# A hybrid convolution and attention step on one core: values moved beside the last convolution, two mixing tiles turned into a seven-product pair

## The chip, the core and the metric

The kernel runs on one core of a Trainium2 chip. The metric is the device time of one execution in microseconds, lower is better; the time before is 889.69 us, the median of three runs from 889.56 to 890.85. Profiles come from one profiled execution, and times within it are counted from the start of its span.

## The reference

One layer acts on 128 prompt tokens and 512 latent tokens, 640 rows in all, with a model width of 1024. Both groups are modulated, and one wide projection gives everything else:

```python
z = h @ w_in
hy, g_h, qkv, g_a, m = jnp.split(z, [3 * D_HYENA, 4 * D_HYENA, 4 * D_HYENA + 3 * D_ATTN, 4 * D_HYENA + 4 * D_ATTN], axis=-1)
hy = short_conv(hy, conv_w, conv_b)
v_h, x1, x0 = jnp.split(hy, 3, axis=-1)
q, k, v = [t.reshape(B, L, N_HEADS, HEAD_DIM) for t in jnp.split(qkv, 3, axis=-1)]
...
u = v_h * x1
y = jnp.fft.irfft(uf * ff[None], n=n, axis=1)[:, :L]     # long convolution with an implicit filter
y_h = (y + u * d_bias) * x0
...
p_h = (y_h * jax.nn.silu(g_h)) @ w_bh
p_a = (y_a * jax.nn.silu(g_a)) @ w_ba
m_h, m_a = jnp.split(jax.nn.sigmoid(m), 2, axis=-1)
out = (m_h * p_h + m_a * p_a) @ w_out
x = layer_norm(ALPHA * x + gate * out)
```

y_a is softmax attention with 16 heads: the latent tokens see a window of 8 rows by 16 columns and a cache of 128 context keys, the prompt sees itself. The prompt's keys and values (new_k, new_v) are outputs too.

## The kernel before

**Tiles.** Activations lie transposed: the modulated input h as eight slabs of 128 channels by 640 tokens, split into a high part hH and a low part hL. A weight tile is 1024 by 128 and gives 128 channels of one projection. A product is made of three passes (high by high weight, low by high weight, high by low weight), so a plain tile is 8 slabs x 3 passes x 2 halves of 320 tokens = 48 matmuls of 320 columns. The tile numbers are constants: queries from 32, keys from 40, values from 48, attention gates T_GA from 56, mixing tiles T_MH and T_MA from 64 and 72.

**Pairs.** Two tiles can be made together as a 2 x 2 block product with seven products instead of eight (`pair_tile`). Its products use sums of blocks of h, which are made once, stored to memory (tok_d) and loaded into tiles t2, t3, t1, t4, and sums of weight blocks (s1, s2, s3, s6), which are made per pair by two accumulating transfers on POOL (`summed`) and two additions on DVE (`sum1`, `sum6`). For each product a weight block is split: the high part on ACT (`high`), the low part on DVE (`low`), both into wb, four blocks ahead of PE. The products read, in this order, h, t2, t3, t1, h, t4, h. Each has 4 slabs x 3 passes = 12 matmuls of 320 columns, so a pair has 84 where two plain tiles have 96.

**Stages.** A prologue makes the modulation and h. Then the long convolution runs in four quarters of 256 channels. `weave` sets a list of projections (main) beside the steps of one quarter's convolution (side): `long_conv` forward, `long_conv_back` with the inverse transform (yb, L170 to L172), its transposes on PE (yp, y; L625, L635), the products on DVE (u, L637) and, once both factors are there, the product yu with x0 (`gate_conv`, L471 and L474) that is stored to yu_d. Up to here a scheduler sets the order of the instructions from the order of the program and its own model of their times. The fourth quarter stands beside `hand_over`: the last convolution tiles, values, queries and keys of the first heads, and two mixing tiles (`mix_tile`), whose tanh goes to mh_d. There the pools of the convolution are given up and their memory goes to the attention (`attention_setup`). The tile sg0 of the first gate lies in memory of that kind.

**From the gates on** the order on all engines is the order of the program. `first_gates` makes two plain gate tiles (mm, L182; tanh on ACT L499 and product on DVE L494, into sg0 and sg1), with the split of the first weight blocks between them. Then SP is given: the four copies of a half of h into a contiguous place (hHp, hLp), the loads of the sums of h that are still out, ra1 (the second pair's plain blocks), the bias tiles tm. t2 and t3 are loaded in two halves of two slabs (t2_00 is the high part's first, t2_10 the high part's second, t2_11 the low part's second); the second halves of t2 and t3 wait in the program's text for the convolution's memory. Transfers of SP are put on eight counters in turn, so each transfer also waits until the one eight before it has landed.

**The attention stage** has eight stages; in each, pairs named in a table (HEADS) are the main list, and the steps of one head pair's attention (`attend`) the side list. The pairs of the first stage make the queries and keys of the second heads ("q1") and two gates of the convolution ("h0"). Pairs of later stages make more gates and the mixing tiles ("m"). Their blocks are loaded two pairs ahead (`load_pair(p + 2)`). After it come the projections of both branches, the mixing and the output.

The table that names the pairs, the place of the pairs in the stage, and the gate of the first two tiles:

```python
HEADS = ("q1 h0", "q2 h1 m1", "q3 m2 a2", "q4 h2 m3", "q5 m4 a4", "q6 h3 m5", "q7 a6", "m6 m7")
for _ in mains(j):
    done += 1
    while done in (14, 20, 27) if j == 0 else taken * n_main < done * n_side:
        if next(side, StopIteration) is StopIteration:
            break
```

## Time and profile before

| what | value |
|---|---|
| median of three runs | 889.69 us |
| the profiled execution's own time | 890.32 us |
| its span | 888.5 us |
| instructions | 17140 |
| mean granted clock of the matrix engine | 0.997 |
| last mixing tile, inverse transform, two gates | 347.6 to 354.6, 354.6 to 360.5, 362.2 to 376.6 us |
| first pair | 376.6 to 389.7 us |

PE is the matrix engine, PEld its weight loads, DVE the vector engine, ACT the scalar engine with its function tables, POOL the general engine, SP the engine that issues most transfers. A timeline row gives start, duration, engine, line, operation, output, inputs, shapes and count (x48 joins 48 like instructions), and in brackets the idle time ahead of it with what ended it. A windows row gives the stretch, its length, the engine's busy time and instructions, its mean granted clock, the share of the DMA engines in use, and GB/s. A row of DMA issues gives the size of a transfer and the median time from its issue to its landing.

### The profile page before, as it was taken

How to read it: one execution, taken by the hardware profiler on the slowest of the kernel's cores; microseconds unless marked ns; L12 is line 12 of the kernel's file. 1: busy time of each engine (PE TensorE's matmuls, PEld its weight loads, DVE VectorE, ACT ScalarE, POOL GpSimd, SP SyncE). 2: the span in 40 equal slices, each digit the busy share in tenths (PEclk: the TensorE clock that was granted, in tenths of full speed). 3: DMA queues.
4: the chain of work that ended last, by engine and by line, in shares of the span. 5: the costliest groups of instructions: out<-in, count | busy, mean ns of one | idle time of the engine just before them, and what ended most of it. 6: DMA issues, size and time to landing. Idle time of an engine off the chain costs nothing.

```text
span 888.5 us, 17140 instructions
## 1 busy us (share of the span) xinstructions
PE 869.3 (98%) x6476; PEld 837.8 (94%) x6476; DVE 637.1 (72%) x1215; ACT 450.3 (51%) x956; POOL 192.9 (22%) x216
## 2 busy tenths in 40 slices
PE   8999999999999999999999999999999999999996
PEld 7889999999899999899999999999999999999885
DVE  4897583985687458488867777777877676676666
ACT  4495545644554544467556566666566632243200
POOL 0020001211101021129344334333554200000000
PEclk9999999999999999999999999999999999999998
DMA  8977576878546697798686758665844586446521
GB/s 329 402 211 156 121 158 145 211 197 190 137 100 159 151 222 149 223 337 266 157 248 150 223 154 239 165 190 172 232 128 128 192 305 228 159 160 196 181 86 57
DMA packets 75246, 169.09 MB, mean 190 GB/s; under 512 B 11003, under 2 KB 28667, under 8 KB 75164
## 3 DMA queue, kind: packets, MB, share of 16 engines
q1 hardware_dynamic: 56204, 123.06, 41.7%
q0 software_dynamic: 13632, 39.33, 23.0%
q10 hardware_dynamic: 5328, 5.61, 1.9%
q8 instruction: 51, 0.84, 0.4%
q14 instruction: 31, 0.25, 0.1%
HBM read 143.32 MB, written 23.99 MB: 188 GB/s over the span
## 4 chain that ended last, share of the span: by engine, by line
PE 93%; DVE 4%; ACT 1%; DMA 1%; issue 1%; POOL 0%; SPq 0%; POOLq 0%; DVEq 0%; ACTq 0%
PE mm L182 34%; PE sp L1234 29%; PE out L1513 6%; PE v L656 5%; PE s L1040 2%; PE s L947 2%; PE pt L1031 2%; PE ve L667 1%; DMA t<-tok_d 1%; PE adaT L252 1%; PE yb L171 1%; PE adaT L269 1%; PE yb L172 1%; PE fl L400 1%; PE ut L540 1%
## 5 line engine op out<-in xcount | busy, mean ns | idle before, releaser
L1234 PE MATMUL sp<-t,wb 128*128 128x320 f32 x1008 | 159.5, 311 | 0.4 <-DMA t<-tok_d 0.4
L1234 PEld LDWEIGHTS sp<-t,wb 128*128 128x128 f32 x1008 | 150.3, 188 | 1.3 <-DMA t<-tok_d 0.6
L1234 PE MATMUL sp<-hH,wb 128*128 128x320 f32 x500 | 120.9, 313 | 0.0
L182 PE MATMUL mm<-hH,wh 128*128 128x320 f32 x336 | 83.6, 314 | 5.8 <-ACT hH L328 2.9
L1234 PEld LDWEIGHTS sp<-hH,wb 128*128 128x128 f32 x500 | 86.0, 188 | 2.6 <-issue 2.6
L182 PE MATMUL mm<-hL,wh 128*128 128x320 f32 x336 | 81.6, 311 | 0.4 <-DVE hL L329 0.2
L182 PE MATMUL mm<-hH,wl 128*128 128x320 f32 x336 | 80.9, 311 | 0.4 <-DVE wl L102 0.4
L162 POOL DMA_DIRECT2D wl<-wall x34 | 30.6, 901 | 221.2 <-ACT wl L161 202.4
L1234 PE MATMUL sp<-hL,wb 128*128 128x320 f32 x250 | 77.2, 309 | 0.0
L163 ACT ACTIVATE wh<-raw 128x1024 fp32r<-128x1024 f32 x34 | 36.2, 1064 | 63.0 <-PE mm L182 47.9
L182 PEld LDWEIGHTS mm<-hH,wh 128*128 128x128 f32 x336 | 57.2, 188 | 8.3 <-ACT hH L328 3.6
L1002 POOL TENSOR_SCALAR p<-p,sm 128x384 f32<-128x384 f32 x32 | 54.1, 1789 | 22.2 <-DVE sm L1000 9.4
L1195 DVE TENSOR_TENSOR wb<-s,wb 128x512 fp32r<-128x512 f32 x63 | 45.6, 725 | 18.6 <-ACT wb L1187 18.4
L182 PEld LDWEIGHTS mm<-hL,wh 128*128 128x128 f32 x336 | 57.2, 188 | 1.5 <-DVE hL L329 1.2
L182 PEld LDWEIGHTS mm<-hH,wl 128*128 128x128 f32 x336 | 57.0, 188 | 1.3 <-DVE wl L102 0.9
L1002 POOL TENSOR_SCALAR edge<-edge,sm 128x320 f32<-128x320 f32 x32 | 42.3, 1482 | 62.7 <-DVE sm L1000 62.7
L1187 ACT ACTIVATE wb<-s 128x512 fp32r<-128x512 f32 x63 | 39.6, 631 | 30.4 <-PE sp L1234 18.6
L1234 PEld LDWEIGHTS sp<-hL,wb 128*128 128x128 f32 x250 | 47.0, 188 | 0.0
L1513 PE MATMUL out<-woh,yhs 128*128 128x512 f32 (+1 forms) x176 | 45.7, 373 | 0.0
L1222 DVE TENSOR_TENSOR spare_hHp<-sp,yu 128x320 f32<-128x320 f32 x63 | 30.5, 484 | 16.9 <-PE sp L1234 10.9
L182 PE MATMUL mm<-yhs,wh 128*128 128x320 f32 x224 | 42.1, 309 | 0.0
L1543 POOL TENSOR_TENSOR r<-r,bc 128x64 f32<-128x64 f32 x1 | 0.3, 319 | 174.1 <-ACT r L1542 174.1
(415 smaller groups left out, 2283.2 us busy)
## 6 DMA issues: line engine op xcount, KB each, us to landing
raw<-wall SPq DMA_DIRECT2D x54, 512.0 KB, 3.7
wl<-wall POOLq DMA_DIRECT2D x34, 512.0 KB, 6.3
ra<-wall SPq DMA_DIRECT2D x21, 512.0 KB, 4.8
rb<-wall SPq DMA_DIRECT2D x40, 256.0 KB, 5.4
ada<-wada SPq DMA_DIRECT2D x16, 512.0 KB, 7.7
tm<-bias SPq DMA_DIRECT2D x16, 512.0 KB, 7.2
s<-wall SPq DMA_DIRECT2D x21, 256.0 KB, 5.1
s<-wall POOLq DMA_DIRECT2D x21, 256.0 KB, 4.4
```

The costliest lines, as they stand in the source:

```text
L162: nc.gpsimd.dma_start(wl, a["wall"][i], accum_op=ALU.add)
L163: nc.scalar.activation(wh, raw[:], AF.Copy)
L182: nc.tensor.matmul(ps[hf][:, :HALF], wt[k], x[:, hf * HALF : (hf + 1) * HALF], start=(i == 0 and k == 0), stop=(i == lead[2] and k == NK - ...
L656: nc.tensor.matmul(ps[t // 2][:, t % 2 * 256 : t % 2 * 256 + 256], x[:, k, P * t : P * t + P], wk, start=first and t % 2 == 0, stop=last, ...
L947: nc.tensor.matmul(dst[h], x[rows(h), qs], y[rows(h), ks], start=i == 0, stop=i == 2, skip_group_check=True)
L1002: nc.gpsimd.tensor_scalar_mul(pv, pv, sm[:, 2, c : c + 1])
L1031: nc.tensor.transpose(pt[:, i * P : i * P + P], ps[h][:, c : c + P], ident)
L1187: nc.scalar.activation(made[g][:, 0], block(g), AF.Copy)
L1195: nc.vector.tensor_tensor(made[g][:, 1], block(g), f(made[g][:, 0]), op=ALU.subtract)
L1222: nc.vector.tensor_tensor(c, dst, c if j == 3 else ps["u"], op=ALU.add)
L1234: nc.tensor.matmul(dst, wk, x(xi, k), start=j < 4 and k == 0 and i == 0, stop=k == 3 and i == 2, skip_group_check=True,)
L1513: ins = nc.tensor.matmul(dst, m[k][:, c0 : c0 + P], w[:, c : c + n], start=(first and k == 0), stop=(last and k == 5), skip_group_check=True,)
```

## The change

Three things are done. First, `values(1)`, the values of the second pair of heads, leaves the list beside the third quarter's convolution and is named first in `hand_over`, beside the fourth; the steps that `weave` counts for the third quarter fall by those of values. Second, the function `mix_tile` goes and with it the two plain mixing tiles 64 and 65 in `hand_over`. The loading and splitting of the gate weights (`wraw`, `wtile`), which stood between the halves of these tiles, now follow the keys directly. Third, the table gets "m0" in the first stage, so tiles 64 and 65 become a pair, the 22nd, and the three attention steps of that stage come after its 14th, 24th and 36th step instead of its 14th, 20th and 27th.

```diff
@@ -762,8 +762,9 @@
             yield
 
     for q in range(3):
-        weave(along(chain(quarter_head(q + 1), quarter_tail(q), values((2, 3, 1)[q], v_d)), sums, 6),
-              chain(long_conv(q), braid(long_conv_back(q), filter_spectrum(q + 1))), 6 * NK + N_VALUES, N_CONV + N_BACK + N_FILTER)
+        fill = (values(2, v_d), values(3, v_d), ())[q]
+        weave(along(chain(quarter_head(q + 1), quarter_tail(q), fill), sums, 6),
+              chain(long_conv(q), braid(long_conv_back(q), filter_spectrum(q + 1))), 6 * NK + (N_VALUES if q < 2 else 0), N_CONV + N_BACK + N_FILTER)
     ident = out["ident"]
 
     def rows(h):
@@ -847,6 +848,7 @@
         yield
 
     def hand_over():
+        yield from values(1, v_d)
         yield from quarter_tail(3)
         hwa_stack.close()
         load_sums(0, SUMS[:2])
@@ -854,22 +856,11 @@
         out["slots_q"] = left.enter_context(tc.tile_pool(name="slots_q", bufs=1))
         first_blocks()
         yield from chain(values(0), queries(0), keys(0))
-        yield from mix_tile(0)
-        last_mix = mix_tile(1)
-        yield next(last_mix)
         for i in range(2):
             wraw(T_GA + i)
-        yield from last_mix
         for i in range(2):
             early[T_GA + i] = wtile(T_GA + i, "dma")
         load_a(0)
-
-    def mix_tile(n):
-        th = row(yhp, "yh", f"mx{n}")
-        for hf, p in enumerate((yield from proj(T_MH + n, eng="dma"))):
-            nc.scalar.activation(th[:, CS[hf]], p[:, :HALF], AF.Tanh, scale=0.5)
-        nc.scalar.dma_start(mh_d[n], th[:])
-        yield
 
     def first_gates():
         yield from gate_a(0)
@@ -1300,7 +1291,7 @@
         return pair_tile(p, use)
 
     N_PAIR = 14
-    HEADS = ("q1 h0", "q2 h1 m1", "q3 m2 a2", "q4 h2 m3", "q5 m4 a4", "q6 h3 m5", "q7 a6", "m6 m7")
+    HEADS = ("q1 h0 m0", "q2 h1 m1", "q3 m2 a2", "q4 h2 m3", "q5 m4 a4", "q6 h3 m5", "q7 a6", "m6 m7")
     MAKE = dict(a=gates_a, h=gates_h, q=queries_keys, m=mix)
 
     def tiles_of(item):
@@ -1380,7 +1371,7 @@
             done = taken = 0
             for _ in mains(j):
                 done += 1
-                while done in (14, 20, 27) if j == 0 else taken * n_main < done * n_side:
+                while done in (14, 24, 36) if j == 0 else taken * n_main < done * n_side:
                     if next(side, StopIteration) is StopIteration:
                         break
                     taken += 1
```

What each engine is given, where the prediction looks. The first place is PE, from the last transposes of the fourth quarter's convolution (y6, y7) on; mm56 is the first gate tile, sp0_0 the first product of the first pair. Words in brackets name the engines and transfers that an instruction waits for. Before:

```order
L635 MATMUL y6_4042<-pack2_380,ye3_3927 128x128 [waits PE_49]
L635 MATMUL y6_4042<-pack2_380,ye3_3927 128x128 x3
L635 MATMUL y7_4076<-pack2_380,ye3_3927 128x128 [waits PE_49]
L635 MATMUL y7_4076<-pack2_380,ye3_3927 128x128 x3
L182 MATMUL mm56_0_4318<-hH_85,wh56_4287 128x320 [waits Activation_49]
L182 MATMUL mm56_1_4319<-hH_85,wh56_4287 128x320 [waits Activation_49]
L182 MATMUL mm56_0_4318<-hL_87,wh56_4287 128x320
L182 MATMUL mm56_1_4319<-hL_87,wh56_4287 128x320
L182 MATMUL mm56_0_4318<-hH_85,wl56_4288 128x320 [waits DMASW0_49]
```

Now:

```order
L635 MATMUL y6_3946<-pack2_380,ye3_3798 128x128 [waits PE_49]
L635 MATMUL y6_3946<-pack2_380,ye3_3798 128x128 x3
L635 MATMUL y7_3981<-pack2_380,ye3_3798 128x128 [waits PE_49]
L635 MATMUL y7_3981<-pack2_380,ye3_3798 128x128 x3
L1225 MATMUL sp0_0_4348<-hH_85,wb0_4250 128x320 [waits DVE_49,Activation_49]
L1225 MATMUL sp0_0_4348<-hL_87,wb0_4250 128x320
L1225 MATMUL sp0_0_4348<-hH_85,wb0_4250 128x320 [waits DVE_49]
```

The two gate tiles have moved up into the place of the two mixing tiles, ahead of the inverse transform, and the first pair follows the transposes directly.

The same place on ACT; yep3 is the last eviction of the inverse transform, mx the mixing tiles' tanh, sg0 the first gate's, wb0 to wb2 the high parts of the first pair's weight blocks. Before:

```order
L621 ACTIVATE yep3_3928<-yb3_2_4003 128x256 [waits PE_49]
L870 ACT_TABLE_LOAD
L870 ACTIVATE mx0_4161<-mm64_0_4169 128x320 [waits DMASW2_49]
L870 ACTIVATE mx0_4161<-mm64_1_4170 128x320
L871 DMA mh_d_77<-mx0_4161 128x640 [waits DMAHW6_49,Activation_49]
L870 ACTIVATE mx1_4222<-mm65_0_4230 128x320 [waits DVE_49]
L870 ACTIVATE mx1_4222<-mm65_1_4231 128x320
L871 DMA mh_d_77<-mx1_4222 128x640 [waits DMAHW0_49,Activation_49]
L499 ACTIVATE sg0_4317<-mm56_0_4318 128x320 [waits DVE_49,PE_49]
L499 ACTIVATE sg0_4317<-mm56_1_4319 128x320 [waits PE_49]
L1187 ACTIVATE wb0_4372<-ra0_4297 128x512 [waits DMAHW5_49,DMASW7_49]
L1187 ACTIVATE wb1_4377<-s1_0_4375 128x512 [waits DMASW0_49,DVE_49]
```

Now:

```order
L621 ACTIVATE yep3_3799<-yb3_2_3905 128x256 [waits PE_49]
L499 ACT_TABLE_LOAD [waits DVE_49,PE_49]
L499 ACTIVATE sg0_4195<-mm56_0_4196 128x320 [waits Activation_49]
L499 ACTIVATE sg0_4195<-mm56_1_4197 128x320
L1178 ACTIVATE wb0_4250<-ra0_4175 128x512 [waits DMAHW2_49,DMASW3_49]
L1178 ACTIVATE wb1_4255<-s1_0_4253 128x512 [waits DMASW6_49,DVE_49]
L1178 ACTIVATE wb2_4258<-s2_0_3764 128x512 [waits DMASW4_49]
L499 ACTIVATE sg1_4261<-mm57_0_4262 128x320
L499 ACTIVATE sg1_4261<-mm57_1_4263 128x320
```

Before, the table of the tanh was loaded without a wait and served the mixing tiles first. Now its first user is the gate's tanh into sg0, and the load carries the wait of that tanh, for DVE and PE. Of the rows of the built program, the DVE instruction that brings the counter to the value waited for is the last product of yu7 (L474), the last reader of the convolution tile in whose memory sg0 lies; the PE instruction is the last transpose of y7.

The second place is SP, at the end of the hand-over. t2_10 waits for the inverse transform (PE) in both. Before, with rows left out:

```order
L63 DMA ra0_4297<-wall 128x1024 [waits DMAHW5_49,DMAHW2_49,Activation_49]
L63 DMA t2_10_4302<-tok_d_81 128x640 [waits DMAHW7_49,PE_49,Pool_49]
L63 DMA t2_11_4304<-tok_d_81 128x640 [waits DMASW6_49]
L63 DMA s2_1_4307<-wall 128x512
L63 DMA rb1_4306<-wall 128x512 [waits DMAHW3_49]
...
L63 DMA t3_10_4311<-tok_d_81 128x640 [waits DMAHW5_49]
L63 DMA t3_11_4313<-tok_d_81 128x640 [waits DMAHW6_49]
L63 DMA hH_85<-hHp_86 128x320 [waits DMAHW7_49,PE_49]
...
L63 DMA t1_00_4446<-tok_d_81 128x640 [waits DMAHW3_49,DMASW2_49,Activation_49]
L63 DMA t1_01_4448<-tok_d_81 128x640 [waits DMAHW4_49,DVE_49]
...
L63 DMA t4_00_4456<-tok_d_81 128x640 [waits DMAHW0_49,DMASW2_49]
...
L63 DMA t4_11_4462<-tok_d_81 128x640 [waits DMAHW3_49,DMASW3_49,DMASW1_49]
```

Now:

```order
L63 DMA ra0_4175<-wall 128x1024 [waits DMAHW4_49,DMAHW2_49,Activation_49]
...
L63 DMA hH_85<-hHp_86 128x320 [waits PE_49]
...
L63 DMA t1_00_4324<-tok_d_81 128x640 [waits DMAHW0_49,DMASW2_49]
L63 DMA t1_01_4326<-tok_d_81 128x640 [waits DMAHW1_49,DVE_49]
L63 DMA t2_10_4180<-tok_d_81 128x640 [waits DMAHW2_49,PE_49,Pool_49]
L63 DMA t2_11_4182<-tok_d_81 128x640 [waits DMAHW3_49,DMASW6_49]
L63 DMA s2_1_4185<-wall 128x512 [waits DMAHW4_49]
L63 DMA rb1_4184<-wall 128x512 [waits DMAHW5_49]
...
L63 DMA t3_10_4189<-tok_d_81 128x640 [waits DMAHW7_49]
L63 DMA t3_11_4191<-tok_d_81 128x640 [waits DMAHW0_49]
...
L63 DMA t1_11_4330<-tok_d_81 128x640 [waits DMAHW2_49]
...
L63 DMA t4_11_4340<-tok_d_81 128x640 [waits DMAHW7_49,DMASW1_49]
```

The four copies inside h, which wait for the end of the gates on PE, and the loads t1_00 and t1_01 now stand ahead of t2 and t3. The DVE instruction for which t1_01 waits is the product of yu6 (L474). Of the eight counters, t1_11 now waits for that of t2_10, and t4_11 for that of t3_10.

On DVE the rows keep their order. Up to the last instruction of the first keys, the rows of PE, ACT, DVE and POOL, values of the second pair among them, are the same in the same order as before.

## The prediction

> **What bounds the kernel now.** I read the page's busy times and the chain that ended last first, then the windows, then each engine's timeline around 345 to 390 us, where the change lies, and last the waits and the DMA issues there.
>
> ```profile
> PE 869.3 (98%) x6476; PEld 837.8 (94%) x6476; DVE 637.1 (72%) x1215; ACT 450.3 (51%) x956; POOL 192.9 (22%) x216
> PE 93%; DVE 4%; ACT 1%; DMA 1%; issue 1%; POOL 0%; SPq 0%; POOLq 0%; DVEq 0%; ACTq 0%
> 400.00:500.00 100.00, 99.96 (x776) 1.00 0.77 216
> ```
>
> PE is busy for 98% of the span and makes 93% of the chain; in attention (third row, 400 to 500 us) it is idle for 0.04 us in 100, at full clock. So a matmul removed there is worth its whole cadence, and every idle microsecond of PE is paid in full. The question is only what PE has to wait for after the change. PE now, around the hand-over:
>
> ```profile
> 347.58 0.31 PE L182 MATMUL mm<-hH,wh 128*128 128x320 f32 x1
> ...
> 354.62 0.27 PE L170 MATMUL yb<-ph,dftH 128*128 128x256 f32 x1
> ...
> 360.73 1.04 PE L635 MATMUL y<-pack,ye 128*128 128x128 f32 x8
> 362.20 0.75 PE L182 MATMUL mm<-hH,wh 128*128 128x320 f32 x2 [0.44 <-ACT mx L870]
> 362.79 0.46 PE L182 MATMUL mm<-hL,wh 128*128 128x320 f32 x2
> ...
> 376.58 0.31 PE L1234 MATMUL sp<-hH,wb 128*128 128x320 f32 x1
> ...
> 387.10 1.00 PE L1234 MATMUL sp<-t,wb 128*128 128x320 f32 x5 [0.42 <-DMA t<-tok_d]
> ...
> 389.79 0.33 PE L947 MATMUL s<-k,q 64*128 64x128 f32 x2
> ```
>
> The second mixing tile runs from 347.58 to 354.62, its 48 matmuls at 0.1467 us each. The last inverse transform and its transposes follow, then from 362.20 the two first gates, and at 376.58 the first pair (sp0), which ends about 389.70.
>
> **The change, part by part.** *Count.* A pair is seven products of 12 matmuls, 84 for 96, of the same 320 columns. Twelve matmuls at 0.1467 us: **-1.76 us**.
>
> *Values of the second pair.* The instruction rows are the same in the same order on all engines up to the last matmul of the first keys, whichever generator names the values. I take 0. Were they really moved, PE at that place would lose the third convolution's filler and the fourth would gain it; both lists keep PE full, so I leave it at 0 on either side.
>
> *Gates in the mixing tiles' place.* This is the real move: PE does the gates before the transposes, and sp0 right behind them. Until now 14 us of gates lay between the convolution's last product and sp0. Other engines at that point:
>
> ```profile
> 363.96 1.42 DVE L474 TENSOR_TENSOR yu<-x,u 128x64 f32<-128x64 f32 x4
> 370.06 0.88 DVE L494 SCALAR_TENSOR_TENSOR sg<-sg,mm 128x320 f32<-128x320 f32 x2 [4.68 <-ACT sg L499]
> 370.91 0.69 DVE L1195 TENSOR_TENSOR wb<-ra,wb 128x512 fp32r<-128x512 f32 x1
> ...
> 382.09 0.49 DVE L1222 TENSOR_TENSOR spare_hHp<-sp,yu 128x320 f32<-128x320 f32 x1 [0.37 <-DMA ra<-wall]
> 382.49 0.68 DVE L1177 TENSOR_TENSOR s<-s,rb 128x512 f32<-128x512 f32 x1
> ```
> ```profile
> 360.42 1.28 ACT L870 ACT_TABLE_LOAD   x1
> 361.71 0.77 ACT L870 ACTIVATE mx<-mm 128x320 f32<-128x320 f32 x2
> ...
> 369.59 0.77 ACT L499 ACTIVATE sg<-mm 128x320 f32<-128x320 f32 x2 [4.08 <-PE mm L182]
> 370.24 0.63 ACT L1187 ACTIVATE wb<-ra 128x512 fp32r<-128x512 f32 x1
> ```
>
> In the new order the table load, and with it the gate's tanh, waits for DVE: the gate's home sg0 is memory of the convolution, free only when the last L474 product is done, here at 363.96 + 1.42 = 365.38 (its inputs, the transposes at 360.73, do not move). Before, ACT loaded the table at 360.42, beside those transposes. Behind the tanh stand, on ACT, the high of the first weight block, and on DVE the gate product and the block's low; sp0's first matmul waits for the product and the high, its third for the low. From the tanh's start to the low's end the trace has 369.59 to 370.91 + 0.69 = 371.60, 2.01 us. So: 365.38 + 1.28 (table) + 2.01 = **368.67** for the third matmul. It could have gone at about 361.9 (transposes' last issue near 361.6, two matmuls more). The hole is 6.8 us; before, the same place cost 0.9 (361.9 against the gates' third matmul at 362.79). Net **+5.9**. The second block's low comes two blocks later on the same two engines, 0.25 after PE wants it: +0.25. The wait at 387.10 goes, since its transfer has time in this hole; with its matmuls' restart I count -0.65. Chain alone: -1.76 + 5.9 + 0.25 - 0.65 = +3.75, which is the floor, sp0 ending at 389.70 - 14.08 (two tiles of 48) + 5.5 = 381.1.
>
> *The load queue.* The transfers that sp0 reads, on SP:
>
> ```profile
> 360.05 0.80 SPq L63 DMA_DIRECT2D t<-tok_d  x2
> 360.90 0.42 SPq L63 DMA_DIRECT2D s<-wall  x1
> 361.37 0.91 SPq L63 DMA_DIRECT2D rb<-wall  x2
> 362.32 7.34 SPq L63 DMA_DIRECT2D t<-tok_d  x2
> ...
> 374.89 2.19 SPq L63 DMA_DIRECT2D t<-tok_d  x4
> 377.69 2.97 SPq L63 DMA_DIRECT2D t<-tok_d  x4
> ```
> ```profile
> SPq L63 <- PE yb L172: 11.0, 1, 11.0
> ```
>
> SP stood 11.0 us until the inverse transform freed the buffer, then issued t2 at 360.05, 16.5 us ahead of sp0. In the new order the four copies inside h and the loads t1_00, t1_01 stand ahead of t2, and t1_01 waits for the product yu6 (L474, first half of the row: 363.96 + 0.71 = 364.67). All behind it is held: t2_10 goes at 365.2 instead of 360.05, and at 0.45 us an issue (0.80 for two, 0.91 for two) s2_1 at 366.1, t3_10 at 367.4, t3_11 at 367.9. Each transfer also waits for the one eight before it: t1_11 for t2_10, t4_11 for t3_10. How long they take is the open cost:
>
> ```profile
> t<-tok_d SPq DMA_DIRECT2D x2, 320.0 KB, 3.5
> s<-wall SPq DMA_DIRECT2D x1, 256.0 KB, 5.4
> ```
> ```profile
> t<-tok_d SPq DMA_DIRECT2D x4, 320.0 KB, 7.0
> ```
> ```profile
> t<-tok_d SPq DMA_DIRECT2D x12, 320.0 KB, 6.4
> s<-wall POOLq DMA_DIRECT2D x1, 256.0 KB, 7.8
> ```
>
> The first two rows are the issues of 360 to 361 us, the quiet bound, the third those of 377.5 to 380.6, the crowded one, the last two the medians over 358 to 385. After the change all of it goes out in one burst behind 364.7, with two stores of yu and two accumulating loads besides, so I take the crowded ends: t3_10 lands at 367.4 + 6.4 to 7.0 = 374, t4_11 goes then and lands at **381.0**. PE wants it for the eighth matmul of the sixth product, at the floor near 378. Five matmuls of that product and twelve of the next remain, 2.5 us: sp0 ends at **383.5**. A second way there: s2_1 (366.1 + 5.4 = 371.5), its accumulating load 7.8, s1 0.68, a low 0.69 and a subtraction 0.49, all ahead of sp0's last product: 381.2, and 1.76 for that product: 383.0. They agree. Net: +12.32 (84 matmuls that now lie in sp0's attention part) - (389.70 - 383.5) = **+6.1**, rounded up to +6.3 for the t1_11 that is held by t2_10.
>
> Bounds: quiet loads put t4_11 at 367.4 + 3.5 + 3.5 = 374.4, no wait, so the floor stands (+3.75); the crowded value for every link, t1_11 included (365.2 + 7.0 + 7.0 = 379.2, PE wanting it at 374.9), puts sp0's end at 385.2: +7.8.
>
> *The clock.*
>
> ```profile
> 880.00:884.00 4.00, 0.21 (x2) 0.81 0.00 0
> 884.00:888.50 4.50, 0.00 (x0) 0.50 0.34 117
> ```
>
> After the last matmul (880.2) the granted clock is 0.50 from 884 on, and a mean of 0.81 over four microseconds puts the fall at 882.5, 2.3 us after PE fell idle. A hole of 6.8 us is longer. How soon the clock comes back no row shows; if it takes as long as the fall, 2.3 us at half speed hold eight matmuls, +1.2 (none: 0; twice as long: 2.4). In the forecast the later wait for t4_11 swallows it.
>
> The Trainium skill says of this ("TensorE: Matmul & The Clock Gate", Part 1: The HAM clock gate) that an idle window of about 3.4 us halves the clock and that about as much sustained work restores it. The trace agrees that idleness halves it, sooner here (2.3 us); by the page the loss is 12 matmuls, an estimate of +1.76 in place of 1.2, and nothing in the forecast, as it is swallowed too.
>
> *The new pair itself and the tail.* The 84 matmuls come in attention's first stage with the row of 400 to 500 as cover; DVE is at 72% and SP's loads for it are 1.5 MB in 12 us beside a share of 0.77. Before, PE lost 0.42 us there. I take 0; up to +3 if the next pair's blocks come late behind the burst.
>
> Sum on the profiled execution, 890.32 us (span 888.5 and 1.8 outside it, taken as unchanged): 896.6. The median of the runs is 0.63 lower, so **889.69 + 6.3 = 896.0 us**.
>
> **The rivals.** *Only the chain* (0.15): the loads land in 3.5 us each, the hole is the chain's alone and the clock's fall is no longer swallowed: 889.69 + 3.75 + 1.2 = 894.6. For it speaks the quiet row; against it, that the burst is denser than that of 377.5.
>
> The Trainium skill ("DMA: Bandwidth & Descriptors", Anatomy of one DMA) has a fit of 2.0 us plus bytes over 436 GB/s, an estimate of 2.75 us for 320 KB. By it this rival would hold. The trace has 3.5 to 7.0 for that size, so here queueing decides.
>
> *Later pairs starve too* (0.12): the clock's loss is not swallowed and the second pair's blocks, queued behind t4, stop PE again: 6.3 + 1.2 + 2 (a value between none and the 5.4 us of one late 256-KB load) = +9.5: 899.2. Against it: two pairs are loaded ahead.
>
> *The other side, faster* (0.05): the tanh does not truly wait for yu7's product (the wait I read as one for sg0's memory ends at an earlier count), the table is loaded beside the transposes as at 360.42, and PE goes on at 362. Then -1.76 and -0.65 remain: 887.3. This decides if the hole is below 0.6 us; for it speaks that ACT's own gap is short today, against it the written wait.
>
> *No change* (0.06): a hole of 2 to 4 us, as when DVE does the gate's share ahead of the convolution's products, is paid by the saving: 890.
>
> **How the numbers follow.** The forecast (0.62) is 894.8 to 898; 0.2%, 1.8 us, is about what a measurement of this kernel can tell from no change. All but the last two rivals are slower by more. The range of 893.0 to 899.3 takes in the floor +3.75, less 0.4 for rows that vary, and the starved pairs, and leaves out the two last rivals and some of the extremes. Faster 0.05, same 0.06, slower 0.89.
>
> **What would show it.** On PE's timeline a hole of 6 to 7 us behind the transposes near 361.6, put down to ACT's tanh or weight high or DVE's sg or low; the table load after yu's last product, at about 365.4; the transfer t behind the four copies held on SP until DVE's yu (L474), at 364.7, and t2 behind it; several microseconds of sp's matmuls waiting for tok_d within the first pair; a granted clock below 1.00 between 364 and 372; 12 matmuls fewer. I am wrong if PE goes on within 2 us of the transposes, if the transfers land before PE asks, or if the extra time appears after 400 us.

## The result, and the profile after

| what | before | after |
|---|---|---|
| median of the runs | 890.04 us (889.56 to 890.85, 4 runs) | 902.14 us (901.36 to 903.45, 4 runs) |
| ratio | | 1.013, 95% interval 1.0107 to 1.0152 |
| span of the profiled execution | 888.5 us | 900.2 us |
| mean granted clock | 0.997 | 0.991 |

The change makes the kernel 12.1 us slower. The forecast was 6.3 us slower, in a range that ends at 9.6: the direction was right, the size was not. The busy times and the chain of the kernel after:

```profile
PE 872.1 (97%) x6464; PEld 840.2 (93%) x6464; DVE 646.1 (72%) x1229; ACT 451.0 (50%) x960; POOL 191.9 (21%) x216
PE 92%; DVE 4%; DMA 2%; ACT 1%; issue 1%; SPq 0%; POOL 0%; POOLq 0%; DVEq 0%; ACTq 0%
```

PE has the 12 matmuls less (6464 for 6476) and is nevertheless busy for 2.8 us longer: some of its matmuls ran slower. DMA is 2% of the chain for 1%. The time was lost in one place. From 400 us on, the windows of PE show no idle time:

```profile
400.00:500.00 100.00, 100.00 (x778) 1.00 0.73 203
```

PE's timeline after, from the last transposes of the convolution (y) to the first score matmul (s), with the rows of sp0 between that carry a wait or show the cadence:

```profile
360.95 1.04 PE L635 MATMUL y<-pack,ye 128*128 128x128 f32 x8
368.26 0.63 PE L1225 MATMUL sp<-hH,wb 128*128 128x320 f32 x1 [6.27 <-ACT wb L1178]
...
370.22 0.47 PE L1225 MATMUL sp<-hHp,wb 128*128 128x320 f32 x1
370.48 0.47 PE L1225 MATMUL sp<-hLp,wb 128*128 128x320 f32 x1
...
371.67 2.82 PE L1225 MATMUL sp<-t,wb 128*128 128x320 f32 x18
375.27 0.41 PE L1225 MATMUL sp<-t,wb 128*128 128x320 f32 x1 [0.77 <-DMA t<-tok_d]
376.09 2.76 PE L1225 MATMUL sp<-t,wb 128*128 128x320 f32 x17 [0.41 <-DMA t<-tok_d]
...
382.47 0.39 PE L1225 MATMUL sp<-t,wb 128*128 128x320 f32 x1 [1.86 <-DVE spare_hHp L1213]
383.99 1.21 PE L1225 MATMUL sp<-t,wb 128*128 128x320 f32 x6 [1.14 <-DMA t<-tok_d]
385.61 1.70 PE L1225 MATMUL sp<-t,wb 128*128 128x320 f32 x5 [0.41 <-DMA t<-tok_d]
...
389.61 0.33 PE L938 MATMUL s<-k,q 64*128 64x128 f32 x2
```

sp0 ends where it ended before: the score matmuls start at 389.61, before at 389.79. So the two mixing tiles, 14.08 us of matmuls, were taken out ahead of this point, and nothing came back. The pair that was put into the attention stage costs its 84 matmuls in full, 12.32 us, and the sum of the two, 12.32 - 0.18 = 12.1, is the result.

PE's waits for transfers in sp0 (us in total, times, longest):

```profile
PE sp L1225 <- DMA t<-tok_d: 2.7, 4, 1.1
```

What stands in the place of the 14.08 us is in these rows: a hole of 6.27 us behind the transposes, eleven first matmuls that start 0.27 us apart (370.22 to 370.48 is one such step) instead of 0.147, waits for t1 at 375.27 and 376.09, a wait of 1.86 us for DVE's subtraction, waits of 1.14 and 0.41 us for t4. The windows of PE show the same stretch beside the transfers (the columns are the length, PE's busy time and matmuls, its clock, the share of the DMA engines and GB/s). Before:

```profile
361.00:366.00 5.00, 4.56 (x32) 1.00 0.86 257
366.00:371.00 5.00, 5.00 (x36) 1.00 1.07 388
371.00:376.00 5.00, 5.00 (x37) 1.00 0.97 253
376.00:381.00 5.00, 5.00 (x37) 1.00 0.96 299
381.00:386.00 5.00, 5.00 (x36) 1.00 1.02 397
386.00:391.00 5.00, 4.58 (x38) 1.00 1.04 403
```

After:

```profile
361.00:366.00 5.00, 0.99 (x10) 0.87 0.07 5
366.00:371.00 5.00, 2.74 (x9) 0.50 0.94 311
371.00:376.00 5.00, 3.91 (x23) 0.95 1.03 401
376.00:381.00 5.00, 4.52 (x29) 1.00 1.07 315
381.00:386.00 5.00, 1.99 (x8) 0.91 1.05 388
386.00:391.00 5.00, 5.00 (x35) 0.74 1.01 326
```

Before, the DMA engines are nearly full for the whole of these 30 us (shares of 0.86 to 1.07), while PE works. The prediction took flight times of transfers from this stretch, but not how full the engines were in it. After, they stand nearly idle for the first five and are full from then on, and PE waits beside them. The clock falls twice: behind the hole (0.87 and 0.50 in the first two rows), and again behind the waits for DVE and t4 (0.91 and 0.74 in the last two).

The transfers, as SP issues them after the change, and the medians from issue to landing for the four of t4 (372.4 to 375.9 us):

```profile
351.73 14.43 SPq L63 DMA_DIRECT2D t<-tok_d  x4
...
368.40 2.06 SPq L63 DMA_DIRECT2D t<-tok_d  x4
...
372.55 3.06 SPq L63 DMA_DIRECT2D t<-tok_d  x4
```
```profile
t<-tok_d SPq DMA_DIRECT2D x4, 320.0 KB, 10.3
```

SP is held in the first row, which lasts 14.43 us, as forecast. The last of t4 goes out at 375.29 and, with 10.3 us of flight, lands at 385.6, where the row at 385.61 shows PE waiting for it. Before, the last t4 went out at 380.08 and landed at 387.05, by the row at 387.10 with its wait of 0.42. So t4 goes out 4.8 us sooner than before and lands only 1.5 us sooner, because its flight is 10.3 us for 7.0. The last landing is at nearly the same time in both kernels, and PE's 14 us more or less ahead of it do not matter. (Before, the four copies that stand ahead of t1 on SP waited for a point within the gates, not for their end: the first of them goes at 370.61, and the gates end at 376.6.)

### The profile page after: what moved, and what is told of

Read it like the earlier page. It is cut to its first block, busy times and chain, and to the rows that moved or that the text cites. A ratio compares the mean times of both kernels' runs of the same rounds, so it can differ in the third digit from the quotient of the medians.

```text
span 900.2 us, 17158 instructions
## 1 busy us (share of the span) xinstructions
PE 872.1 (97%) x6464; PEld 840.2 (93%) x6464; DVE 646.1 (72%) x1229; ACT 451.0 (50%) x960; POOL 191.9 (21%) x216
## 4 chain that ended last, share of the span: by engine, by line
PE 92%; DVE 4%; DMA 2%; ACT 1%; issue 1%; SPq 0%; POOL 0%; POOLq 0%; DVEq 0%; ACTq 0%
PE mm L182 33%; PE sp L1225 30%; PE out L1504 6%; PE v L656 5%; PE s L1031 2%; PE s L938 2%; PE pt L1022 2%; DMA t<-tok_d 2%; PE ve L667 1%; PE adaT L252 1%; PE adaT L269 1%; PE yb L171 1%; PE fl L400 0%; PE ut L540 0%; PE fl L401 0%
## 5 line engine op out<-in xcount | busy, mean ns | idle before, releaser
L1225 PE MATMUL sp<-t,wb 128*128 128x320 f32 x1056 | 168.1, 312 | 4.6 <-DMA t<-tok_d 2.7
L1225 PEld LDWEIGHTS sp<-t,wb 128*128 128x128 f32 x1056 | 158.1, 189 | 6.4 <-DMA t<-tok_d 3.7
L1225 PE MATMUL sp<-hH,wb 128*128 128x320 f32 x524 | 128.0, 316 | 6.3 <-ACT wb L1178 6.3
L1225 PEld LDWEIGHTS sp<-hH,wb 128*128 128x128 f32 x524 | 91.1, 190 | 9.4 <-ACT wb L1178 6.5
L182 PE MATMUL mm<-hH,wh 128*128 128x320 f32 x312 | 78.0, 315 | 4.4 <-ACT zs L484 2.4
L1225 PE MATMUL sp<-hL,wb 128*128 128x320 f32 x262 | 81.5, 311 | 0.0
L182 PE MATMUL mm<-hL,wh 128*128 128x320 f32 x312 | 76.3, 313 | 0.2 <-DVE hL L329 0.2
L182 PE MATMUL mm<-hH,wl 128*128 128x320 f32 x312 | 75.8, 312 | 0.4 <-DVE wl L102 0.4
L163 ACT ACTIVATE wh<-raw 128x1024 fp32r<-128x1024 f32 x32 | 34.0, 1063 | 55.6 <-PE mm L182 40.5
L993 POOL TENSOR_SCALAR p<-p,sm 128x384 f32<-128x384 f32 x32 | 51.6, 1733 | 24.0 <-PE sp L1225 10.2
L182 PEld LDWEIGHTS mm<-hL,wh 128*128 128x128 f32 x312 | 53.4, 189 | 1.2 <-DVE hL L329 0.9
L101 ACT ACTIVATE wh<-raw 128x1024 fp32r<-128x1024 f32 x15 | 15.8, 1058 | 46.7 <-PE mm L182 33.6
```

Source lines behind the costliest of these rows:

```text
L163: nc.scalar.activation(wh, raw[:], AF.Copy)
L182: nc.tensor.matmul(ps[hf][:, :HALF], wt[k], x[:, hf * HALF : (hf + 1) * HALF], start=(i == 0 and k == 0), stop=(i == lead[2] and k == NK - ...
L993: nc.gpsimd.tensor_scalar_mul(pv, pv, sm[:, 2, c : c + 1])
L1225: nc.tensor.matmul(dst, wk, x(xi, k), start=j < 4 and k == 0 and i == 0, stop=k == 3 and i == 2, skip_group_check=True,)
```

## The experiments

Each kernel was timed beside the kernel before on the same chip. To compare traces I use one length, D: from PE's row of the last transposes (y, L635) to the first score matmul. It is 389.79 - 360.73 = 29.06 us before and 389.61 - 360.95 = 28.66 after. A kernel with the added pair should stand 12.32 + (D - 29.06) above the kernel before. "Queue", "home", "late bias" and "fillers" are explained where they first come. Where an expectation calls t1 or t4 the second pair's, it is mistaken: they are sums of h that all pairs read; only the weight blocks (ra1, rb1, s2_1) belong to a pair.

| kernel | D | from D | median less before | ratio (95%) |
|---|---|---|---|---|
| the change | 28.66 | +11.9 | +12.1 | 1.013 (1.0107 to 1.0152) |
| e1, values alone | - | - | +0.15 | 0.9999 (0.9986 to 1.0013) |
| e8, pair added, plain tiles kept | 28.29 | +11.6 | +12.4 | 1.014 (1.0125 to 1.0156) |
| e3, home | 31.42 | +14.7 | +14.0 | 1.0155 (1.0131 to 1.0179) |
| e2, queue | 25.59 | +8.9 | +8.9 | 1.0103 (1.0079 to 1.0127) |
| e4, queue and home | 25.57 | +8.8 | +9.0 | 1.0104 (1.008 to 1.0128) |
| e6, late bias | 27.82 | +11.1 | +10.5 | 1.0117 (1.0102 to 1.0132) |
| e7, t4 first | 29.86 | +13.1 | +13.2 | 1.0143 (1.0126 to 1.016) |
| e10, no t4 | 23.79 | +7.1 | +8.0 | 1.0088 (1.0059 to 1.0117) |
| e11, queue, home, stores on ACT, late bias | 26.14 | +9.4 | +10.4 | 1.0109 (1.0086 to 1.0131) |
| e5, 40 and 32 fillers | 28.25 | +11.5 | +11.8 | 1.0139 (1.0117 to 1.0162) |
| e9, 20 fillers, second place | 27.32 | +10.6 | +10.4 | 1.0111 (1.0087 to 1.0135) |
| e13, queue, late bias, no t4 | 24.22 | +7.5 | +6.1 | 1.0068 (1.0053 to 1.0083) |
| e14, the same and 40 fillers | 25.64 | +8.9 | +8.6 | 1.0097 (1.008 to 1.0114) |
| e15, queue, late bias, 40 fillers | 27.56 | +10.8 | +8.1 | 1.009 (1.0075 to 1.0105) |
| e16, queue, late bias, no t1 or t4 | 21.44 | +4.7 | +6.0 | 1.0071 (1.0054 to 1.0087) |
| e17, the same and 40 fillers | 20.66 | +3.9 | +4.8 | 1.0055 (1.004 to 1.007) |

The two columns agree within 1.4 us, for e15 within 2.8; D is one execution. Beside e13 to e15 the kernel before had a median of 891.71, beside the others 889.75 to 890.22, so these three read some 1.8 us too low in the column of medians and in that of ratios. The D of the kernel before varies as well: e1, which issues the same instructions in the same order, has 389.01 - 360.73 = 28.28 us and no wait for t4. Taken from there, the column from D is 0.8 us higher for every kernel.

### The parts of the change: e1 and e8

e1 is the kernel before with the values alone moved:

```diff
-        weave(along(chain(quarter_head(q + 1), quarter_tail(q), values((2, 3, 1)[q], v_d)), sums, 6),
+        fill = (values(2, v_d), values(3, v_d), ())[q]
+        weave(along(chain(quarter_head(q + 1), quarter_tail(q), fill), sums, 6),
 ...
     def hand_over():
+        yield from values(1, v_d)
         yield from quarter_tail(3)
```

> The kernel before with only the first part of the change: the values of the second pair of heads are named beside the fourth quarter's convolution, the two plain mixing tiles stay. Theory (the instruction order does not change, so the values cost nothing and the whole loss is the missing cover behind the convolution): 890.0 us, within 0.5 of the kernel before. Rival (the moved values take cover from the third convolution and cost some of the 12 us): 892 or more, with new idle time of PE before 340 us.

It measured 890.1 us, ratio 0.9999. The move of the values costs nothing, as the prediction had it.

e8 is the kernel before with the pair added and the two plain mixing tiles left in place, so that they are made twice:

```diff
-    HEADS = ("q1 h0", "q2 h1 m1", ...
+    HEADS = ("q1 h0 m0", "q2 h1 m1", ...
-                while done in (14, 20, 27) if j == 0 ...
+                while done in (14, 24, 36) if j == 0 ...
```

> The kernel before with the new pair in the first stage and its attention steps at 14, 24, 36, but with the two plain mixing tiles still computed in the hand-over (their result is computed twice). PE does 96 matmuls more than the changed kernel. Theory (the two tiles were cover that the place needs, and taking their 14.1 us out gives nothing back): 889.95 + 12.3 = 902.2, the same as the changed kernel within 0.5. Rival (the new pair costs more than its matmuls, through its loads and DVE in the first stage, and the hand-over is less bad than it looks): above 903.5.

It measured 902.66 us, against 902.14 of the change. This is the plainest of the runs: with 96 matmuls more, the kernel takes the same time (it also lacks the move of the values, which costs nothing by e1). The window of PE in this kernel:

```profile
361.00:386.00 25.00, 24.38 (x166) 1.00 0.97 329
```

PE is busy for 24.38 of 25 us at full clock, and sp0 ends at 389.75. Taking the plain tiles out of it saves PE 14.1 us of work and not one of time. What the added pair costs, 12.4 us, is its matmuls (12.32) and no more.

### The hole: e3

The prediction put the hole down to the gate's tile sg0, whose memory is the convolution's. e3 gives the even gate tiles a pool of their own that is opened ahead of the others, and moves another tile into their place:

```diff
+        sgp = ac.enter_context(tc.tile_pool(name="sgp", bufs=1, side="right"))
 ...
-        spare.append(sp.tile([P, HALF], F32, tag="yu", name="yu")[:])
+        spare.append(at.tile([P, HALF], F32, tag="yu", name="yu")[:])
 ...
+    def sg_tile(j):
+        return (at if j % 2 else sgp).tile([P, NT], F32, tag=f"sg{j % 2}", bufs=1, name=f"sg{j}")
 ...
-        out[f"sg{j}"] = sg = at.tile([P, NT], F32, tag="sg", bufs=2, name=f"sg{j}")
+        out[f"sg{j}"] = sg = sg_tile(j)
```

> The changed kernel with the first gate's tile in a pool of its own outside the convolution's memory, so its table load and tanh wait for nothing; the load queue stays late. Theory (the queue sets the end of the first pair): PE starts the pair near 365.6 instead of 368.3, but the convolution's products come later on DVE, t1_01's wait ends near 368 and t4 lands later: 903 to 905, no gain. Rival (the hole of the tanh is the cost): 899.4 or less, as the pair's start moves by 2.7 us.

It measured 903.92 us, 1.8 more than the change. PE's waits (us in total, times, longest):

```profile
PE sp L1229 <- DMA t<-tok_d: 7.0, 7, 2.4
...
PE sp L1229 <- ACT wb L1182: 1.3, 1, 1.3
```

And SP's row of t1_00 to t2_11, which is 14.43 us long in the change:

```profile
351.09 17.75 SPq L63 DMA_DIRECT2D t<-tok_d  x4
```

The wait of 6.3 us for ACT falls to 1.3, so the memory was its cause. But DVE now makes the gate product, a split and a sum of weight blocks ahead of the convolution's last products, so SP is held by one of them for 3.3 us longer, everything behind it goes out later, and PE waits 7.0 us for transfers instead of 2.7. A shorter hole with later loads is a loss.

### The load queue and what shares it: e2, e4, e6, e7, e10, e11, e12

e2 issues the second halves of t2 and t3 and the second weight blocks ahead of the copies of h and of t1, as it was before:

```diff
-    pinned[0] = True
-    load_sums(1, SUMS[:1])
-    sums_of_second = load_b(1)
-    load_sums(1, SUMS[1:2])
-    pinned[0] = False
 ...
     with tc.manual_schedule(engines=engines):
         for _ in first_gates():
             pass
+        load_sums(1, SUMS[:1])
+        sums_of_second = load_b(1)
+        load_sums(1, SUMS[1:2])
         sums_of_second()
```

> The changed kernel with the load queue put back: the second halves of t2 and t3 and the second pair's blocks go out ahead of the four copies inside h and of t1, as in the kernel before; the tanh still waits for the last product of the convolution. Theory (hole of the tanh 6.3 us stays, but t4's last part is issued near 369 instead of 375.3 and lands before PE asks for it): the first pair ends near 382.3, 895 us (894 to 896.5), waits for tok_d and for DVE's subtraction under 0.5 us, one fall of the clock instead of two. Rival (the tanh's hole and the clock carry the loss, the queue does not matter): 901 to 902.

It measured 898.82, 3.3 us better than the change and 3.8 worse than expected, and so between the theory and the rival. e4 takes the home of e3 as well:

> Both of the last two: queue put back and first gate's tile outside the convolution's memory. Theory: with the loads early the hole decides, the pair ends near 381.6 and the time is 894.3 (893 to 896), a little under the queue alone. Rival (two independent costs that add up): the queue's gain plus 2.7, about 892.

It measured 898.93, against both expectations and no better than e2 alone: PE starts the pair 5 us earlier and ends it at the same time. The second half of the burst goes out no sooner in e2: t1 and t4 stand behind the convolution's last products all the same. SP in e2:

```profile
369.76 3.38 SPq L63 DMA_DIRECT2D t<-tok_d  x4
...
373.94 4.06 SPq L63 DMA_DIRECT2D t<-tok_d  x3
```

The first row is the four transfers of t1, the last is three of t4. This trace lies 2.15 us later than that of the change (its first yp row is at 362.83 for 360.68). The last t1 goes out at 372.04, which is 369.9 on the clock of the change, for 370.10 there; t4 is held between its parts until the stores of yu have landed.

e6 issues the bias tiles (two transfers of 512 KB) behind the third pair's blocks instead of behind t4. They lie behind t4 in the queue, so by the order of SP alone they could not delay it:

```diff
-        biases[0] = [bias_tile(h) for h in range(2)]
 ...
                 done += 1
+                if j == 0 and done == 11:
+                    biases[0] = [bias_tile(h) for h in range(2)]
```

> The changed kernel with the two bias tiles (tm0, tm1, 1 MB), which are issued right behind t4, issued after the third pair's blocks instead. Theory (t4's transfers took 10 us because all that is under way shares the engines): t4's last part lands 1.5 to 2.7 us earlier, 899.5 to 900.7. Rival (what is issued later does not slow what was issued earlier): t4 lands as before, 902.

It measured 900.76, 1.4 us less. The issues of 370.5 to 376 us:

```profile
t<-tok_d SPq DMA_DIRECT2D x4, 320.0 KB, 9.5
```

t4 takes 9.5 us for 10.3. The same median is 10.2 in e5 and 10.5 in e9, which issue these transfers in the order of the change, so the step is more than chance here: what is issued behind a transfer slows it all the same.

e7 issues t4 ahead of the second pair's plain blocks (ra1):

```diff
-        load_a(1)
         load_sums(0, SUMS[3:])
         load_sums(1, SUMS[3:])
+        load_a(1)
```

> The changed kernel with t4 issued ahead of the second pair's plain block ra1 (512 KB). Theory: t4's last part is issued about 1 us earlier with half a megabyte less ahead of it and lands 1 to 2 us earlier, but ra1 lands later by as much, and the split of its block and the subtraction behind it on DVE hold the sixth product: 901 to 902.5, little gain. Rival (t4's landing alone sets the end): 900 to 900.5.

It measured 903.38, slower than the change and than expected. Of PE's waits:

```profile
PE sp L1225 <- DVE spare_hHp L1213: 3.2, 1, 3.2
PE sp L1225 <- DMA t<-tok_d: 2.3, 5, 0.5
```

The waits for the sums of h shorten (2.3 us for 2.7), the wait for DVE's subtraction grows (3.2 for 1.9): in the order of DVE a split of ra1 stands ahead of it. What goes first only chooses which of the two is late.

e10 leaves the loads of t4 out; its products read the tiles of t3:

```diff
-        load_sums(0, SUMS[3:])
-        load_sums(1, SUMS[3:])
+        tok["t4"] = tok["t3"]
```

> The changed kernel without the four loads of t4 (1.3 MB): the products that should read t4 read t3's tiles, so the loads are left out and that part of the result is another one; PE's work is the same. Theory (what the DMA engines have to move behind the convolution sets the first pair's end): the next thing late is DVE's subtraction behind the second pair's accumulated block, near 382; the pair ends near 385.7, 898.2 (897 to 899). Rival (the hole of the tanh and the half speed alone are the cost): 901 to 902.

It measured 897.94, 4.2 us less, as expected.

e11 takes queue, home and late bias together and has ACT issue the last two stores of yu, which t1 and t4 wait for:

```diff
-            nc.gpsimd.dma_start(yu_d[n], y)
+            (nc.scalar if n > 5 else nc.gpsimd).dma_start(yu_d[n], y)
```

> The changed kernel with all repairs: load queue as before, first gate's tile outside the convolution's memory, the last two stores of yu issued by ACT so that POOL's accumulating loads do not stand ahead of them, the two bias tiles behind the third pair's blocks. Theory (some 6 MB have to move between 360 us and the sixth product at some 0.37 MB per us): gains over queue and home together (898.9) by the megabyte that is moved out of the way and the stores, 896.5 (895.5 to 898), still slower than the kernel before. Rival (the waits were only matters of order and are gone now): 891 or less.

It measured 900.29, worse than e2 and than expected. With the home of e3 DVE ends the product that the first of these stores waits for only at 369.84; the store goes out at 369.86, and PE waits 4.1 us for tok_d.

e12 is the kernel before with the bias tiles ahead of t4, to see whether that kernel has any room at this place:

```diff
+        biases[0] = [bias_tile(h) for h in range(2)]
         load_sums(0, SUMS[3:])
         load_sums(1, SUMS[3:])
-        biases[0] = [bias_tile(h) for h in range(2)]
```

> The kernel before, where nothing is changed but that the two bias tiles (1 MB) are loaded ahead of t4 and not behind it. Theory (the DMA engines are as full there before the change, share 0.86 to 1.07 from 361 to 391, and t4's last part lands at 387.05 just when PE asks for it, so that place has no slack): t4 lands 2 to 2.7 us later and the time grows by as much, 892.3 (891.5 to 893). Rival (the wait of 0.42 us there is chance and the loads have slack): 890.0 to 890.6.

It measured 891.6 (890.63 to 894.86, 10 runs) for 889.93, ratio 1.0017 (1.0001 to 1.0032). That lies in the range of the theory, but its interval (0.1 to 2.8 us) also takes in the rival. In the profiled execution, which took 893.85, PE stops where it did not before:

```profile
387.46 0.38 PE L1234 MATMUL sp<-t,wb 128*128 128x320 f32 x1 [1.36 <-ACT wb L1187]
```

The row names ACT, whose weight high ends at 387.36; the first part of t4 lands at 387.32 (before: 384.62), so both were late.

### The clock: e5 and e9

e5 fills PE's hole with 40 matmuls that nobody reads, and sets 32 more ahead of the sixth product:

```diff
+        if q == 3:
+            for _ in range(40):
+                nc.tensor.matmul(outp[:, :HALF], hH[:, 0, :P], hH[:, 0, :HALF], start=True, stop=True, skip_group_check=True)
+            yield
 ...
+            if g == 5:
+                dm = aux("dm")
+                for _ in range(32):
+                    nc.tensor.matmul(dm[:, :HALF], hH[:, 0, :P], hH[:, 0, :HALF], start=True, stop=True, skip_group_check=True)
```

> The changed kernel with idle work for PE in its two holes: 40 matmuls whose result nobody reads behind the last transposes (5.9 us in the hole of 6.3) and 32 ahead of the first pair's sixth product (4.7 us in the waits of 380.4 to 385.6). So the granted clock does not fall; no wait is shorter. Theory (the loss of the first fall is swallowed by the wait for t4's last part, landing 385.6; that of the second, 17 matmuls in 4.0 us in place of 2.5, is not): 1.5 us less, 900.6 (900 to 901.4). Rival (half speed is a cost of its own in both places, 4.4 us in all): 898 or less. Other rival (the clock does nothing): 902.

It measured 902.04, the same as the change. PE's rows:

```profile
375.14 0.42 PE L1233 MATMUL sp<-t,wb 128*128 128x320 f32 x1 [1.43 <-DMA t<-tok_d]
...
380.94 4.85 PE L1229 MATMUL dm<-hH 128*128 128x320 f32 x32
385.62 1.92 PE L1233 MATMUL sp<-t,wb 128*128 128x320 f32 x12
```

The first fillers keep the clock up, and PE waits 1.43 us for t1 instead of 0.77: what the full clock saves is given back at t1. The second fillers were too many: they ended at 385.6 and held up the first seven matmuls of the product. e9 has 20 in that place and none in the hole:

> The changed kernel with 20 idle matmuls (2.9 us, nobody reads them) ahead of the first pair's sixth product only, so that PE is not idle long enough there for the clock to fall a second time; unlike the 32 of the earlier run they end before t4's second part lands (383.9), so no matmul of the product is pushed behind them. Theory (behind t4's landing at 385.6 the rest, 17 matmuls, takes 2.5 us in place of 4.0): 900.6 (900 to 901.3). Rival (the second fall costs nothing either): 902.

It measured 900.34, 1.8 us less than the change. The last rows of sp0:

```profile
385.68 0.99 PE L1229 MATMUL sp<-t,wb 128*128 128x320 f32 x5 [0.39 <-DMA t<-tok_d]
...
388.36 0.33 PE L938 MATMUL s<-k,q 64*128 64x128 f32 x2
```

The last part of t4 lands at the same time as in the change (385.68 for 385.61), and the rest of sp0 takes 2.7 us instead of 4.0. So the second fall of the clock costs some 1.3 us in this trace; the medians differ by 1.8, but the intervals of the two ratios overlap.

### Without the late transfers: e13, e14, e16, e17, and the best of all: e15

e13 takes the queue of e2, the late bias of e6 and the missing t4 of e10 together. e14 adds the 40 fillers in the hole.

> The changed kernel with the load queue put back, the bias tiles late, and without the four loads of t4 (its products read t3's tiles, so the loads are left out and that part of the result is another one). Theory (with the transfers out of the way the hole and the half speed behind it are left): the pair's third matmul at 368.7, 82 matmuls of 0.1467 us and 1.5 to 3.2 us of half speed, end near 383: 895.5 (894.5 to 896.5). Rival (something else in the pair's start is late): 897 or more.

> The same with 40 idle matmuls in the hole, so that the clock does not fall. Theory: what is left is the hole alone, the forecast's floor of +3.75: 893.7 (893 to 894.5), 1.5 to 3 less than without them. Rival (the clock is swallowed here too): the same as without them.

e13 came to 897.85 us, a ratio of 1.0068, e14 to 900.33 and 1.0097: with fillers it is slower, against both theories. For e13 the microseconds and D speak for the rival, the ratio for the theory. In e13 PE starts at half speed, has the full clock again from 374.1, and waits 0.47 and 0.36 us for t1. In e14 it starts at full speed, and at t1:

```profile
376.13 1.01 PE L1229 MATMUL sp<-t,wb 128*128 128x320 f32 x5 [1.34 <-DMA t<-tok_d]
...
379.17 1.70 PE L1229 MATMUL sp<-t,wb 128*128 128x320 f32 x5 [0.85 <-DMA t<-tok_d]
```
```profile
376.00:381.00 5.00, 3.22 (x13) 0.76 1.03 407
```

PE comes early and waits in pieces until the last part of t1 lands, 18.1 us behind the transposes (18.0 in e13), and in these pieces the clock falls. Until then nothing is won, and after it ten matmuls run slow. So t1 was late too, and the 40 fillers could not show what the first fall costs. e16 and e17 leave out t1's loads as well (its products read the tiles of t2):

```diff
-        load_sums(0, SUMS[2:3])
-        load_sums(1, SUMS[2:3])
         load_a(1)
+        tok["t1"] = tok["t2"]
         tok["t4"] = tok["t3"]
```

> Leaves out the second pair's t1 and t4 loads (its third and fourth value products read the t2 and t3 tiles), with the queue order and the late bias tiles of the run before; output is not the reference's. In e13_few_loads PE still waited 0.47 and 0.36 us for t1, and sp0 ended at 384.78. Theory A (with the transfers gone the clock alone is left): PE starts at about 367.9 at half speed for some 6.5 us, does 24 matmuls in them and the other 62 at 0.147 us, sp0 ends at about 383.5: 6.3 us before 389.79, against the pair's 12.3: +6.0, ratio about 1.0068. Theory B (something else than transfers and clock holds the later products): sp0 ends at 384.8 or later, ratio 1.008 or more.

> The same without the second pair's t1 and t4 loads, and 40 idle matmuls of 128x320 in PE's hole ahead of sp0 so that the clock has no reason to fall; output is not the reference's. Theory A: PE starts at about 368.4 at 0.147 us for each of 86 matmuls, no wait for a transfer, sp0 ends at 381.2 to 381.7: 8.1 to 8.6 us before 389.79, net +3.7 to +4.2, ratio about 1.0045, and 1.8 to 2.3 us below e16, which is the first fall's price once nothing swallows it. Theory B: no difference between the two (under 0.7 us), as the fall is swallowed by some other wait.

e16 measured 895.78, e17 894.58. Neither waits anywhere in sp0 but at its start. Windows of e16:

```profile
366.00:371.00 5.00, 2.77 (x10) 0.50 1.05 343
371.00:376.00 5.00, 5.00 (x34) 0.95 1.06 331
```

Half speed ends 3.2 us after PE's first matmul here, half of what was expected, and costs 0.8 us of D (21.44 to 20.66; 1.2 us by the medians), between the two expectations. That is the price of a short fall: in e13 half speed lasted 6.3 us from PE's start. That e16's ratio is the expected one is luck, since sp0 ends 1.2 us sooner than was worked out. What is left in e17 is the hole: 20.66 - (29.06 - 14.08) = 5.7 us of D (6.5 with the D of e1), 4.8 us over the kernel before by the medians. By the ratios e13 (1.0068) and e16 (1.0071) are alike, so what t1 costs rests on D and on 897.85 against 895.78 us, measured on two chips.

e15 is what could be kept of all this with the computation whole: queue, late bias and 40 fillers.

> The changed kernel, all its loads and its whole result, with the load queue put back, the bias tiles late and the 40 idle matmuls. Theory (t1's and t4's landing set the end whatever PE's clock): 898 (897 to 899), no better than the queue alone by more than 1.5. Rival (hole and clock are what is left): 894 or less.

It measured 899.78, a ratio of 1.009 (1.0075 to 1.0105), above the range of its theory and far from the rival. No version with the 22nd pair came near the kernel before, and even e17, without 2.6 MB of its loads (eight of 320 KB), did not.

## Why the prediction was wrong in size

The path of the forecast was right: a hole, a held queue, and t4 landing last. Two of its terms were not: the flight of t4, taken as 7.0 us, and a second fall of the clock, taken as nothing. Together they are the 6 us that are missing.

**Right.** The 12 matmuls are gone (-1.76). The values cost nothing (e1). The table load waits for yu's last product and the hole is 6.27 us, its third matmul at 368.99 for a forecast of 368.67:

```profile
365.63 1.28 ACT L499 ACT_TABLE_LOAD   x1 [5.00 <-DVE yu L474]
```

SP is held until 364.9 (forecast 364.7). The pair itself runs at its cadence, and nothing is lost after 400 us, so the rival of later pairs that starve falls; so do those of the other side and of no change, and that of the chain alone, since the loads took up to 10.3 us and not 3.5. The chain alone was priced at +3.75, and e17, which is nearly that, measured +3.9 by D and +4.8 by the medians. Two figures beside the sum are off and carry no weight: SP's loads for a pair are 1.3 MB (512 and three times 256 KB), not 1.5, and between the convolution's last product (365.38) and sp0 (376.58) lay 11.2 us of the gates, not 14.

**Wrong: the flight of t4, in the step on the load queue.** t4_11 was to go at 374, when t3_10 had landed, and land at 381.0, 7.0 us later. The link was as forecast (t3_10 landed at 375.22, t4_11 went at 375.29), but the flight took 10.3 us. It landed at 385.57, 4.6 us late: 1.3 by the issue, 3.3 by the flight. That is 4.6 of the 6.1 us by which sp0 ends later than the forecast of 383.5. The "crowded" price came from the kernel before, where some of the same transfers had gone out 5 us sooner. Adding up, from the issues and landings of both traces, what had been issued and had not landed when the last t4 went out, I get about 2 MB before and 3 MB after, an estimate; the engines were full both times (0.96 to 1.07), so it is the bytes in the queue and not the share that tell the two flights apart. The upper bound of the step used the same 7.0 and so was no bound. With 1 MB moved behind, the flight is shorter (e6: 9.5 us for 10.3), and that PE paid for this landing is shown by e10, which leaves t4 out and takes 4.2 us less.

The Trainium skill's fit for one transfer ("DMA: Bandwidth & Descriptors", Anatomy of one DMA), by which 320 KB would be an estimate of 2.75 us, is off here by a factor of 3.7. The Trainium skill gives it there for transfers that the general engine (POOL) issues, and these go out on SP; the prediction did not say so. The quietest load of this size, t1's first in the change, took 3.0 us.

**Wrong: the sum of two limits.** The prediction counted the wait at 387.10 as 0.65 us that the change gives back. It was a sign that transfers were about as late as PE could bear. The wait itself is chance: in e1 and e8, whose transfers are those of before, it is absent, and the last t4 lands 0.4 and 0.5 us ahead of the matmul that reads it. So either way the place had about half a microsecond of slack, and the 0.65 were not there to be had. The windows of before were there to be read: 253 to 403 GB/s and engines at 0.86 to 1.07 for 30 us, some 10 MB (the six rates by 5 us each). Here matmuls taken away ahead of the last landing gave nothing back, and e8 beside the change shows just this. Of the kernels tried, only those without the loads of t1 and t4 came near the floor of +3.75.

**Wrong: the second fall of the clock, which the prediction put at nothing.** The first was seen, and rightly taken as swallowed (e5, e14). That the waits which swallow it would themselves bring the clock down was not. The 17 matmuls behind t4 took 4.0 us (385.61 to 389.61) for 2.5: +1.5, which with the 4.6 is the whole of the 6.1. e9 measured it at 1.3 to 1.8.

The Trainium skill ("TensorE: Matmul & The Clock Gate", Part 1: The HAM clock gate, under its heading on oscillation) warns of gaps of more than about 3.4 us. The trace has the second fall without one: the longest single gap there is 1.86 us, in a window where PE is busy for 1.99 of 5 us.

**Right, but not what decided: DVE.** The wait of 1.86 us at 382.47 is for a subtraction behind a sum of the second pair's weight blocks, whose accumulating transfer was late. DVE's rows:

```profile
380.66 0.69 DVE L1168 TENSOR_TENSOR s<-s,rb 128x512 f32<-128x512 f32 x1 [3.04 <-DMA s<-wall]
...
381.88 0.48 DVE L1213 TENSOR_TENSOR spare_hHp<-sp,spare_hHp 128x320 f32<-128x320 f32 x1
```

The prediction had this second way, and timed it near t4's landing (381.2 for 381.0). In the change it is over before the last t4 lands, so its wait cost nothing of its own there; it is part of the idle time behind which the clock fell. A wait for DVE is also why t4 first (e7) does not help: of the transfers in the burst, several are wanted at once.

Of the 13.7 us that were lost of the 14.08, the runs give: the hole 5.7 (e17), the first fall 0.8 (e16 less e17), t1 2.8 (e13 less e16), and 4.4 for t4, the order of the queue, the bias tiles and the second fall together (the change less e13). That last split isn't clean: e2, e6, e9 and e10 alone give 3.1, 0.8, 1.3 and 4.9 us of D, more than the 4.4 when added, since they overlap. With the D of e1 for the kernel before, the loss and the hole are each 0.8 us larger. Left open is also whether t1 and t4 could go out before the convolution's last products, with other memory for them; that wasn't tried.

## What to carry to other kernels

Work taken off the busiest engine gives time back only up to the next landing, so look at the DMA windows beside it: engines near full for tens of microseconds, and a last landing within a microsecond of its reader, mean that two limits are in balance. A flight time read from a trace holds for the bytes that were in flight there; if a change packs the same transfers closer, count the bytes ahead and beside. A plain test before all others is to put the removed work back and keep the rest: if the time stays the same, the work was cover.

## What was not expected of the hardware

- A transfer of 320 KB took 3.5 us in the quiet issues of before and 10.3 in the burst. A transfer issued later slowed those before it (9.5 us for 10.3 with 1 MB moved behind).
- After holes of the same length (6.3 us) half speed did not last equally long: until 3.2 us after PE's first matmul in the change, and until 6.3 us after it in e13. In the 14 traces whose clock fell between 355 and 395 us it changed only at steps of 3.41 us. Windows of PE on these steps, the change and then e13:

```profile
361.25:364.66 3.41, 0.74 (x7) 1.00 0.00 0
368.08:371.49 3.41, 3.23 (x11) 0.50 0.99 382
381.73:385.14 3.41, 1.53 (x7) 1.00 1.03 403
```
```profile
367.30:370.71 3.41, 2.84 (x10) 0.50 1.09 327
370.71:374.12 3.41, 3.41 (x15) 0.50 1.05 317
```

  Behind the first and the third row the clock fell, behind the second and the last it came back, behind the fourth it stayed low. In those 14 traces it fell 20 times, each time behind a step in which PE was busy for 0.2 to 1.73 of the 3.41 us, and it kept full speed only behind steps with 1.7 us and more. It came back behind steps with 2.8 us and more, and stayed low with up to 2.8. So PE's share in such a step tells it, and not the length of one gap: about half a step to keep full speed, over 0.8 to get it back. The 2.3 us that the prediction read behind the last matmul are then no fixed delay. All this is read from the traces alone; no run set the share on purpose.
- Fillers that keep the clock up can cost time: 40 of them added 1.4 us of D (e14 against e13), since PE then waited in pieces, and the clock fell later, where nothing swallowed it.
